# Chunk inputs by way of DRAM, and a new order of the mixer, in a hybrid decoder step

## The chip, the core and the metric

The kernel runs on one core of a Trainium2 chip. The metric is device microseconds of one execution, the median of several. PE is TensorE, DVE VectorE, ACT ScalarE, POOL GpSimd and SP SyncE, whose queue carries nearly all loads.

## The reference

One inference step of two trunk layers over 320 tokens (a prompt of 256 and eight samples of eight), each layer a half feed-forward, a mixer, a second half feed-forward and a gated input embedding:

```python
# Each layer (pre-RMSNorm everywhere, plain residual adds):
#   x += 0.5 * SwiGLU_1(rms(x))
#   z  = rms(x) @ w_in  -> [u (SSM_W) | q (ATTN_W) | k (KV_W) | v (KV_W)]
#   y_ssm  = GLU(Re(C h_t) + D u_t), h_t = Abar h_{t-1} + Bbar u_t   (32 groups x 16 ch, 64 complex states each)
#   y_attn = sliding-window (128) GQA with per-head sinks
#   x += concat(rms(y_ssm), rms(y_attn)) @ w_out
#   x += 0.5 * SwiGLU_2(rms(x))
#   x += (p[i] @ w_ple_proj) * sigmoid(rms(x) @ w_ple_gate)
def ssm_scan(u, h0, lam_re, lam_im, log_dt, b_re, b_im, c_re, c_im, d, w_glu):
    ...
    bu = jnp.einsum('gnp,blgp->lbgn', b_bar, ug)
    if h0 is not None:
        bu = bu.at[0].add(a_bar * h0)
    a = jnp.broadcast_to(a_bar, (l, SSM_G, SSM_N))
    _, h = lax.associative_scan(_ssm_combine, (a, bu), axis=0)
    y = jnp.einsum('gpn,lbgn->blgp', c, h).real.reshape(bt, l, SSM_W)
```

The scan is done in 40 chunks of eight tokens: what a chunk adds to the state (a product of its inputs with a table `wb` of powers), a scan over the chunks, and the output of a chunk from its own inputs (table `tt`) and from the state ahead of it (table `wc`).

## The kernel before

Features lie on the 128 partitions and the 320 tokens along the free axis. Every weight tile of 128x1024 is loaded by SP, and cut into a high half by ACT (L171, `wh`) and a low half by DVE (L172, `wl`); a product is three matmuls of 128x320 for each block of 128 rows (L206 to L208), 24 for one block of outputs. These long matmuls are nearly all that PE does.

`mix` does the mixer of one layer. A string of operations, `MIXSEQ`, is the order in which its code is written, and so the order of each engine's instructions; a scheduler then moves single instructions within what their tiles allow. A letter is an operation, its number the block: `p` and `q` the projections (`p0` to `p3` are u, 4 to 7 the queries, 8 and 9 key and value), `i` the chunk inputs, `r` the rotation, `v` the transposes of the value, `s` the scores and softmax of one pair of heads, `f` the transposes of the probabilities, `m` their product with the values, `y` the chunk output in its parts, `z` a product of the layer embedding, `t` and `w` loads of tables, `x` the load of the embedding, `g` the GLU, `A` and `S` the output projection.

- A projection ends in an evacuation by DVE that multiplies by the norm: u to `u2` (L682), queries (L686), key and value (L689, and an output `o_kvT` on POOL's queue, L690). PSUM has four kinds of buffers: `pc` (2), `pt` (3), `pa` (2), `po` (1). `p0` to `p7` but 2 and 3, and `z`, use `pc`; `p2`, `p3`, `p8`, `p9`, scores and transposes use `pt`.
- `chunk_in` (`i`) brings u of eight groups to chunk-major form: eight transposes of 128x40 (L699) in two halves, each copied to `X` by ACT (L82, tile `sx`), eight transposes of 40x128 (L704) of X, copied to `U` by ACT, and then 16 products with `wb` (L710), which ACT copies to `Vt`.
- `rotate` (`r`) is ten DVE instructions on eight groups: turn, scan over the chunks (L738), turn back, to `H` (L742) and `fin` (L743).
- `scores` (`s`) is for each of two heads two matmuls (L802, L804) and a masking on DVE (L805), then for the pair two reductions (L810), four exps on ACT (L812), a reciprocal (L814) and two products (L816). POOL writes the sinks ahead of it (L797). `flip` is six transposes (L827) and `mix` six products (L836). The tiles of `s` and of `rotate` take turns in two buffers.
- `y` is 16 products for eight groups (L923), two ACT copies to `sx`, eight transposes (L934) and a GELU on DVE and ACT (L936 to L946).

The tables are made by `prep`, whose steps lie beside the feed-forward ahead of the layer: powers of the state matrix in `pr`, `pi` (tiles `pwr`, `pwi`; POOL clears the first of each, L406, L407, behind a power function of its own, L427), `wc`, a table `tt` written to DRAM by eight copies on POOL's queue (L596, tile `ttd`), and `wb` (L605 to L627) from `q`.

```python
MIXSEQ = 'w0 q0 p3 i0 p2 i2 r0 w1 i3 r2 i1 p8 r3 r1 t1 p9 v t2 p5 t0 e x p4 y0 s0 s1 w2 f0 p6 m0 p7 s2 f1 t3 m1 s3 f2 m2 y0 w3 y0 y1 s4 f3 y1 m3 s5 z0 f4 z1 y1 z2 z3 y2 f5 y2 y3 m4 y3 y2 z4 y3 z5 z6 m5 a g0 g1 A0 n z7 A1 A2 S0 S1 S2 A3 S3'
ABUFS = {"s": 2, "p": 2, "qs": 1, "kc": 1, "vc": 1, "sx": 2, "pj": 1}
PBUFS = {"pa": 2, "pt": 3, "pc": 2, "po": 1}
```

## Time and profile before

| what | before |
|---|---|
| median of 3 runs | 1277.06 us (1277.05 to 1277.24) |
| the profiled execution's own time | 1276.93 us |
| its span | 1275.2 us |
| PE busy | 1257.2 us (99%) |
| DVE busy | 901.4 us (71%) |
| ACT busy | 602.0 us (47%) |
| POOL busy | 69.0 us (5%) |
| chain that ended last | PE 93%, DVE 3%, issue 2%, ACT 1% |
| POOL's queue | 2144 packets, 7.11 MB |
| SP's queue | 72992 packets, 198.50 MB |

The own time of the profiled execution is the span and what lies around it. A matmul's duration is longer than its distance to the next, since matmuls overlap: a long one is listed with 0.31 us, and starts 0.147 after the one ahead. What something costs on PE is read from starts, not from durations. A product of less than 128 rows or columns leaves two records for an instruction in some lines, so 16 products of L710 are 32 records. The mixer of layer 0 runs from 256.2 to 334.2, that of layer 1 from about 883.

### The profile page before, as it was taken

To read this page: it belongs to the slowest core of one execution; us is meant where nothing else is said; L and a number is where in the kernel's file an instruction comes from. 1 tells how busy PE (TensorE), PEld (TensorE's weight loads), DVE (VectorE), ACT (ScalarE), POOL (GpSimd) and SP (SyncE) were. 2 spreads that over 40 slices of the span, in tenths; PEclk is the share of its full clock that TensorE was granted. 3 is DMA by queue.
4 is the path that set the end of the run, shared out by engine and by line. 5 is a ranking of instruction groups with operands and counts; after the bars stand their busy time and mean duration, and the time that the engine had idled before them with its cause. 6 is when DMAs were issued, how large, how long until landed. Compare 5 with 4: busy or idle time off the path is not lost.

```text
span 1275.2 us, 23019 instructions
## 1 busy us (share of the span) xinstructions
PE 1257.2 (99%) x9167; PEld 1230.7 (97%) x9167; DVE 901.4 (71%) x1611; ACT 602.0 (47%) x995; POOL 69.0 (5%) x85
## 2 busy tenths in 40 slices
PE   9999999999999999999999999999999999999996
PEld 8999999988899999999999999999889999999996
DVE  7799677778779987766875555566977755555576
ACT  6443344556764433444654334445485543334454
POOL 2200200010104002000000000000000000000000
PEclk9999999999999999999999999999999999999998
DMA  7646855643254468655444354345422443444351
GB/s 242 216 123 193 298 205 180 229 165 122 77 179 162 128 188 298 222 196 156 167 158 151 117 165 166 131 124 190 177 105 98 151 149 125 147 175 143 114 174 42
DMA packets 75964, 208.72 MB, mean 164 GB/s; under 512 B 9664, under 2 KB 20544, under 8 KB 75856
## 3 DMA queue, kind: packets, MB, share of 16 engines
q1 hardware_dynamic: 72992, 198.50, 46.9%
q0 software_dynamic: 2144, 7.11, 1.5%
q8 instruction: 72, 1.18, 0.4%
q10 hardware_dynamic: 720, 1.64, 0.4%
q14 instruction: 36, 0.29, 0.1%
HBM read 193.62 MB, written 17.79 MB: 166 GB/s over the span
## 4 chain that ended last, share of the span: by engine, by line
PE 93%; DVE 3%; issue 2%; ACT 1%; DMA 0%; POOL 0%; POOLq 0%; SPq 0%; DVEq 0%; ACTq 0%
PE pt L206 18%; PE pt L207 18%; PE pt L208 17%; PE pc L206 11%; PE pc L207 11%; PE pc L208 11%; PE pa L923 1%; PE pa L623 1%; PE po L836 0%; PE pa L273 0%; DVE wl L172 0%; PE pt L827 0%; DVE s L734 0%; DVE s L733 0%; PE pa L934 0%
## 5 line engine op out<-in xcount | busy, mean ns | idle before, releaser
L171 ACT ACTIVATE wh<-wr 128x1024 fp32r<-128x1024 f32 (+3 forms) x370 | 351.9, 953 | 574.7 <-issue 276.7
L206 PE MATMUL pt<-big,wh 128*128 128x320 f32 x1584 | 491.8, 311 | 0.1
L207 PE MATMUL pt<-big,wh 128*128 128x320 f32 x1584 | 490.8, 310 | 0.0
L208 PE MATMUL pt<-big,wl 128*128 128x320 f32 x1584 | 490.3, 310 | 0.0
L172 DVE TENSOR_TENSOR wl<-wr,wh 128x1024 fp32r<-128x1024 f32 (+3 forms) x370 | 402.8, 1091 | 118.0 <-ACT wh L171 116.0
L206 PE MATMUL pc<-big,wh 128*128 128x320 f32 x984 | 307.5, 313 | 0.1
L207 PE MATMUL pc<-big,wh 128*128 128x320 f32 x984 | 305.2, 310 | 0.0
L208 PE MATMUL pc<-big,wl 128*128 128x320 f32 x984 | 305.1, 310 | 0.0
L206 PEld LDWEIGHTS pt<-big,wh 128*128 128x128 f32 x1584 | 297.6, 188 | 2.6 <-issue 1.2
L207 PEld LDWEIGHTS pt<-big,wh 128*128 128x128 f32 x1584 | 297.8, 188 | 0.9 <-DVE big L259 0.6
L208 PEld LDWEIGHTS pt<-big,wl 128*128 128x128 f32 x1584 | 297.7, 188 | 0.1
L206 PEld LDWEIGHTS pc<-big,wh 128*128 128x128 f32 x984 | 185.3, 188 | 1.7 <-issue 0.8
L208 PEld LDWEIGHTS pc<-big,wl 128*128 128x128 f32 x984 | 185.2, 188 | 0.4 <-issue 0.3
L207 PEld LDWEIGHTS pc<-big,wh 128*128 128x128 f32 x984 | 185.3, 188 | 0.3 <-issue 0.3
L322 DVE TENSOR_TENSOR fa<-pt,ft 128x320 f32<-128x320 f32 x88 | 43.1, 490 | 82.4 <-PE pt L208 82.2
L319 DVE TENSOR_TENSOR ft<-pc,r 128x320 f32<-128x320 f32 x87 | 42.2, 489 | 52.5 <-PE pc L208 52.3
L370 DVE SCALAR_TENSOR_TENSOR fd<-pt,r 128x320 f32<-128x320 f32 x64 | 31.5, 491 | 37.0 <-PE pt L208 37.0
L278 POOL TENSOR_TENSOR r<-ms,mhalf 107x3 f32<-107x3 f32 x13 | 15.6, 1202 | 622.8 <-DVE ms L276 622.8
L320 ACT ACTIVATE ft<-ft 128x320 f32<-128x320 f32 x88 | 40.0, 457 | 7.9 <-DVE ft L319 7.7
L327 DVE TENSOR_TENSOR big<-fa,big 128x320 fp32r<-128x320 f32 x88 | 42.7, 486 | 1.1 <-ACT big L326 1.1
L326 ACT ACTIVATE big<-fa 128x320 fp32r<-128x320 f32 x88 | 40.3, 459 | 5.7 <-DVE fa L322 5.3
L254 ACT ACTIVATE big<-xa,prm 128x320 fp32r<-128x320 f32 x64 | 35.5, 559 | 15.8 <-DVE xa L371 9.1
(252 smaller groups left out, 898.6 us busy)
## 6 DMA issues: line engine op xcount, KB each, us to landing
wr<-f2g SPq DMA_DIRECT2D x44, 512.0 KB, 3.3
wr<-f2u SPq DMA_DIRECT2D x44, 512.0 KB, 3.2
wr<-f1g SPq DMA_DIRECT2D x43, 512.0 KB, 3.3
wr<-f1u SPq DMA_DIRECT2D x43, 512.0 KB, 3.3
wr<-f1d SPq DMA_DIRECT2D x32, 384.0 KB, 3.1
wr<-f2d SPq DMA_DIRECT2D x32, 384.0 KB, 3.1
wr<-f1d SPq DMA_DIRECT2D x32, 320.0 KB, 2.9
wr<-win SPq DMA_DIRECT2D x20, 512.0 KB, 4.3
```

Source lines behind the costliest of these rows:

```text
L171: S.activation(h[:, c], raw[:, c], AF.Copy)
L172: lastwl.append(V.tensor_tensor(lo[:, c], raw[:, c], h[:, c].bitcast(F32), op=OP.subtract).ins)
L206: PE.matmul(ps, h[:, c], xh, start=start and k == 0, stop=False)
L207: PE.matmul(ps, h[:, c], xl, start=False, stop=False)
L208: mm = PE.matmul(ps, lo[:, c], xh, start=False, stop=stop and k == n - 1)
L254: S.activation(h, src, AF.Copy, scale=g)
L319: V.tensor_tensor(t, pg, r, op=OP.mult)
L320: S.activation(t, t, AF.Silu)
L322: V.tensor_tensor(a, pu, t, op=OP.mult)
L326: S.activation(h, a, AF.Copy)
L327: V.tensor_tensor(lo, a, h.bitcast(F32), op=OP.subtract)
L370: V.scalar_tensor_tensor(t, pd, 0.5, r, op0=OP.mult, op1=OP.mult)
```

## The change

1. `chunk_in` keeps only the 16 products with `wb` and the copy to `Vt`. The transposes L699 and L704 and the copies to X and U are gone. In their place a new operation `u`, `shuffle`, writes the four blocks of `u2` to a scratch tensor `ud` in DRAM, four copies of 160 KB, and reads it back into `U` in chunk-major form with eight copies, each to 16 partitions in 512 runs of 160 B. All twelve are on POOL's queue.
2. In U the order of the eight tokens of a chunk is turned, and so the rows of `tt` and the powers of `wb` are too. For that `prep` has 16 ACT copies that mirror `pr` and `pi` into `prr` and `pir`.
3. `MIXSEQ` is another. `u` follows p2 and p3; the projections p8, p9, p4 and p5, s0, f0, s1 and m0 stand ahead of the chunk products, which come in pairs around p6; the rotations follow, among the softmaxes.
4. `behind`: once a chunk product is written, the PE instructions of later `p`, `z` and `g` are held behind it in PE's order.

```diff
@@ -32,7 +32,7 @@
 STAT = (0, 107, 213)
 PF = 2
 WB = 4
-MIXSEQ = 'w0 q0 p3 i0 p2 i2 r0 w1 i3 r2 i1 p8 r3 r1 t1 p9 v t2 p5 t0 e x p4 y0 s0 s1 w2 f0 p6 m0 p7 s2 f1 t3 m1 s3 f2 m2 y0 w3 y0 y1 s4 f3 y1 m3 s5 z0 f4 z1 y1 z2 z3 y2 f5 y2 y3 m4 y3 y2 z4 y3 z5 z6 m5 a g0 g1 A0 n z7 A1 A2 S0 S1 S2 A3 S3'
+MIXSEQ = 'w0 q0 p2 p3 u p8 e p9 v p4 s0 p5 f0 i0 t0 r0 i1 w1 r1 p6 i2 t1 r2 s1 i3 w2 r3 x p7 m0 f1 y0 s2 y0 m1 y0 s3 t2 f2 y1 w3 m2 f3 y1 s4 m3 y1 z0 y2 t3 z1 f4 y2 z2 s5 z3 y2 f5 y3 m4 z4 y3 y3 z5 z6 m5 a g0 g1 A0 n z7 A1 A2 S0 S1 S2 A3 S3'
 ABUFS = {"s": 2, "p": 2, "qs": 1, "kc": 1, "vc": 1, "sx": 2, "pj": 1}
 PBUFS = {"pa": 2, "pt": 3, "pc": 2, "po": 1}
 KCUT = 7
@@ -592,14 +592,18 @@
             yield
         src = kt_d[l].rearrange("(p g) c -> p g c", g=G)
         for i in range(8):
-            dst = tt_d[l][(7 - i) * 16 : (8 - i) * 16, :].rearrange("p (g c) -> p g c", c=P)
+            dst = tt_d[l][i * 16 : i * 16 + 16, :].rearrange("p (g c) -> p g c", c=P)
             PO.dma_start(dst, src[:, :, (7 - i) * 16 : (7 - i) * 16 + P])
             if i % 4 == 3:
                 yield
-        V.tensor_copy(q[0:64, 0], pr[0:64])
-        V.tensor_copy(q[64:128, 0], pi[64:128])
-        V.tensor_scalar(q[0:64, 1], pi[0:64], -1.0, None, op0=OP.mult)
-        V.tensor_copy(q[64:128, 1], pr[64:128])
+        prr, pir = st("prr", (P, 8, G)), st("pir", (P, 8, G))
+        for k in range(8):
+            cp(prr[:, 7 - k], pr[:, k])
+            cp(pir[:, 7 - k], pi[:, k])
+        V.tensor_copy(q[0:64, 0, 0:8], prr[0:64])
+        V.tensor_copy(q[64:128, 0, 0:8], pir[64:128])
+        V.tensor_scalar(q[0:64, 1, 0:8], pir[0:64], -1.0, None, op0=OP.mult)
+        V.tensor_copy(q[64:128, 1, 0:8], prr[64:128])
         yield
         for gb in range(4):
             es = []
@@ -635,6 +639,8 @@
         groups = [0]
         tabs = {}
 
+        ud = dram.tile([4 * P, 8, NC], F32, name=f"ud{l}")
+
         def load(kind, gb):
             t = tabs[kind, gb] = tab.tile([P, 8, P], F32, name=nm(kind), tag="tab")
             src = {"wb": wb_d[l][gb], "wc": wc_d[l][gb], "tt": tt_d[l][:, gb * 1024 : (gb + 1) * 1024]}
@@ -690,26 +696,25 @@
                 PO.dma_start(O["kvT"][l, m - 8], t)
                 kv.append(t)
 
+        behind = []
+
+        def shuffle(k):
+
+            for gb in range(4):
+                drain(gb)
+                PO.dma_start(ud[gb * P : gb * P + P], u2[:, gb])
+            src = ud.rearrange("(g p) j c -> j p g c", p=16)
+            for j in range(8):
+                PO.dma_start(U[j * 16 : j * 16 + 16], src[j])
+
         def chunk_in(gb):
-            drain(gb)
-            X = auxt("sx", [NC, 8, 8, 16])
-            for hf in range(2):
-                px = pst("pa")
-                for s in range(4):
-                    PE.transpose(px[:NC, s * P : (s + 1) * P], u2[:, gb, 7 - (hf * 4 + s), :], ident)
-                cp(X[:, :, hf * 4 : hf * 4 + 4, :].rearrange("c g i p -> c i g p"),
-                   px[:NC].rearrange("c (i g p) -> c i g p", i=4, g=8))
-            pu = pst("pa")
-            for g in range(8):
-                PE.transpose(pu[:, g * NC : (g + 1) * NC],
-                             X[:, g].rearrange("c i p -> c (i p)"), ident[:NC, :NC])
-            cp(U[:, gb * 8 : gb * 8 + 8, :], pu[:, : 8 * NC].rearrange("p (g c) -> p g c", g=8))
             pv = pst("pa")
             for g in range(8):
                 for e in range(0, P, 64):
-                    PE.matmul(pv[e : e + 64, g * NC : (g + 1) * NC],
-                              tabs["wb", gb][:, g, e : e + 64], U[:, gb * 8 + g, :],
-                              start=True, stop=True)
+                    mm = PE.matmul(pv[e : e + 64, g * NC : (g + 1) * NC],
+                                   tabs["wb", gb][:, g, e : e + 64], U[:, gb * 8 + g, :],
+                                   start=True, stop=True)
+            behind[:] = [mm.ins]
             cp(Vt[:, gb * 8 : gb * 8 + 8, :], pv[:, : 8 * NC].rearrange("p (g c) -> p g c", g=8))
 
         gr, gi, ect, est, dec = gtab[l]
@@ -985,7 +990,7 @@
         un = [Prompt(m) for m in range(4)] + [Sample(0), Sample(1)]
         co = [chunk_out(gb) for gb in range(4)]
         ops = {
-            "p": proj, "q": proj2, "i": chunk_in, "r": rotate,
+            "p": proj, "q": proj2, "i": chunk_in, "u": shuffle, "r": rotate,
             "v": lambda k: attn_setup(), "s": lambda k: un[k].scores(),
             "f": lambda k: un[k].flip(), "m": lambda k: un[k].mix(),
             "y": lambda k: next(co[k], None), "g": glu,
@@ -996,7 +1001,8 @@
             "A": lambda k: wout("woa", k), "S": lambda k: wout("wos", k),
         }
         for o in seq:
-            ops[o[0]](int(o[1:] or 0))
+            with tc.issue_after(behind[0]) if behind and o[0] in "pzg" else nullcontext():
+                ops[o[0]](int(o[1:] or 0))
         shp = [P, G, 8]
         ft = auxt("s", [P, 2, G, 8])
         V.tensor_tensor(ft[:, 0], h0, gr.unsqueeze(2).to_broadcast(shp), op=OP.mult)
```

Lines from `load` on stand up to six further down in the new file (L710 is L714, L682 L688, L686 L692, L732 to L743 L737 to L748, L802 L807, L805 L810, L816 L821, L827 L832, L923 L928, L934 L939; L797 is L802).

On PE, ahead of a chunk product of layer 0 before (`pa_3258`, `pa_3264` the halves of X, `pa_3270` U of one block, `pt_3356` the key's projection):

```order
L699 MATMUL pa_3258<-ident,big_2998 40x128 [waits PE_49]
L699 MATMUL pa_3258<-ident,big_2998 40x128 x3
L207 MATMUL pt_3356<-big_2831,wh_3092 128x320
L699 MATMUL pa_3264<-ident,big_2998 40x128 [waits Activation_49]
L699 MATMUL pa_3264<-ident,big_2998 40x128 x3
L208 MATMUL pt_3356<-big_2830,wl_3093 128x320
L206 MATMUL pt_3356<-big_2830,wh_3092 128x320
L207 MATMUL pt_3356<-big_2831,wh_3092 128x320
L208 MATMUL pt_3356<-big_2830,wl_3093 128x320
L206 MATMUL pt_3356<-big_2830,wh_3092 128x320
L704 MATMUL pa_3270<-ident,sx_3257 128x40 [waits Activation_49]
L704 MATMUL pa_3270<-ident,sx_3257 128x40 x7
```

and at the first two chunk products now (`big_3018` is U, `big_3019` Vt, `pc_3432` the projection p6):

```order
L841 MATMUL po_3580<-p_3353,vtok_3032 64x128 x4
L841 MATMUL po_3580<-p_3353,vtok_3032 64x128 [waits Activation_49]
L841 MATMUL po_3580<-p_3353,vtok_3032 64x128
L714 MATMUL pa_3364<-big_3018,wb_3009 64x40 [waits DMASW5_49,DMASW4_49,DMASW6_49,DMASW3_49,DMASW7_49,DMASW2_49,DMAHW2_49,DMASW1_49,DMASW0_49]
L714 MATMUL pa_3364<-big_3018,wb_3009 64x40 x15
L714 MATMUL pa_3395<-big_3018,wb_3011 64x40 [waits DMAHW1_49]
L714 MATMUL pa_3395<-big_3018,wb_3011 64x40 x15
L206 MATMUL pc_3432<-big_2627,wh_3270 128x320
L207 MATMUL pc_3432<-big_2628,wh_3270 128x320
L208 MATMUL pc_3432<-big_2627,wl_3271 128x320
```

The products of i0 and i1 stand behind m0 (L841) and directly behind one another; the first waits for the reads from DRAM, the next long matmuls are p6's.

On DVE, the first rotation before (`s_3244`) stands among the evacuation of u (L682) and the cuts of weights:

```order
L172 TENSOR_TENSOR wl_3353<-wr_3350,wh_3352 128x1024 [waits DMAHW6_49,Activation_49]
L732 TENSOR_TENSOR s_3244<-big_3000,ect_877 128x256 [waits Activation_49]
L733 TENSOR_TENSOR s_3244<-big_3000,est_878 64x256
L734 TENSOR_TENSOR s_3244<-big_3000,est_878 64x256
L682 TENSOR_TENSOR big_2998<-pt_3177,r_3119 128x40x8 [waits PE_49]
L737 TENSOR_TENSOR s_3244<-s_3244 128x256 [waits DVE_49]
L172 TENSOR_TENSOR wl_3411<-wr_3408,wh_3410 128x1024 [waits DMAHW7_49,Activation_49]
L738 SCALAR_TENSOR_TENSOR s_3244<-dec_874,s_3244 128x256 [waits DVE_49,Pool_49]
L732 TENSOR_TENSOR s_3244<-s_3244,ect_877 128x256 [waits DVE_49]
L733 TENSOR_TENSOR s_3244<-s_3244,est_878 64x256
L734 TENSOR_TENSOR s_3244<-s_3244,est_878 64x256
L742 TENSOR_TENSOR big_3002<-s_3244 128x8x31 [waits DVE_49]
```

and the end of the third rotation now (`s_3478`), with the softmax of s1 (`s_3489`) and the evacuation of p7 (`pc_3554`):

```order
L810 SCALAR_TENSOR_TENSOR s_3489<-pt_3495,maskp 128x384
L743 SCALAR_TENSOR_TENSOR s_3478<-dec_874,s_3478 128x256 [waits DVE_49]
L815 TENSOR_REDUCE mneg_3499<-s_3489 128x2 [waits DVE_49]
L737 TENSOR_TENSOR s_3478<-s_3478,ect_877 128x256 [waits DVE_49]
L738 TENSOR_TENSOR s_3478<-s_3478,est_878 64x256
L739 TENSOR_TENSOR s_3478<-s_3478,est_878 64x256
L815 TENSOR_REDUCE mneg_3499<-s_3489 128x2
L747 TENSOR_TENSOR big_3021<-s_3478 128x8x31 [waits DVE_49]
L748 TENSOR_TENSOR fin_3022<-s_3478 128x8
L692 TENSOR_TENSOR big_3020<-pc_3554,r_3138 128x320 [waits PE_49]
L737 TENSOR_TENSOR s_3530<-big_3019,ect_877 128x256 [waits DVE_49,Activation_49]
L738 TENSOR_TENSOR s_3530<-big_3019,est_878 64x256
```

Rotations r0 to r2 and the maskings of s1 stand ahead of the evacuation of p7, and r3 (`s_3530`) behind it. On PE the second product of the embedding (`pc_3822`) takes the buffer of p7, and y0's transposes (L939) come behind it:

```order
L207 MATMUL pc_3802<-big_3543,wh_3428 128x320 [waits DVE_49]
L208 MATMUL pc_3802<-big_3543,wl_3429 128x320
L206 MATMUL pc_3822<-big_3543,wh_3428 128x320 [waits DVE_49]
L207 MATMUL pc_3822<-big_3543,wh_3428 128x320
L208 MATMUL pc_3822<-big_3543,wl_3429 128x320
L206 MATMUL pc_3822<-big_3543,wh_3428 128x320
L207 MATMUL pc_3822<-big_3543,wh_3428 128x320
L939 MATMUL pa_3653<-ident,sx_3601 128x40 [waits PE_49,Activation_49]
L939 MATMUL pa_3653<-ident,sx_3601 128x40 x7
```

On ACT, at the first SiLU (L320) of the first feed-forward before:

```order
L239 ACTIVATE sq_264<-xa 128x320 [waits DVE_49]
L171 ACTIVATE wh_391<-wr_389 128x1024 [waits DMAHW2_49,PE_49]
L320 ACT_TABLE_LOAD
L320 ACTIVATE ft_343<-ft_343 128x320 [waits DVE_49]
L171 ACTIVATE wh_446<-wr_444 128x1024 [waits DMAHW6_49,PE_49]
```

and now:

```order
L239 ACTIVATE sq_264<-xa 128x320 [waits DVE_49]
L171 ACTIVATE wh_391<-wr_389 128x1024 [waits DMAHW2_49,PE_49]
L82 ACTIVATE prr_1985<-pwr_434 128x32 [waits Pool_49]
L82 ACTIVATE pir_1986<-pwi_435 128x32 [waits Pool_49]
L320 ACT_TABLE_LOAD
L320 ACTIVATE ft_343<-ft_343 128x320 [waits DVE_49]
L171 ACTIVATE wh_446<-wr_444 128x1024 [waits DMAHW6_49,PE_49]
```

The first pair of mirroring copies stands ahead of the table load and waits for POOL.

## Rows read from the trace of the kernel before

**Rows 1.** Busy us by stretch (x records), granted clock, DMA share, GB/s: projections; the mixer's sum.

```profile
264.50:291.80 27.30, 26.53 (x287) 23.75 (x286) 24.10 (x51) 11.78 (x21) 2.60 (x4) 1.00 0.47 167
...
sum 78.00, PE 76.15 PEld 66.72 DVE 62.74 ACT 50.40 POOL 8.09; mean PE 15.23 PEld 13.34 DVE 12.55 ACT 10.08 POOL 1.62
```

**Rows 2.** Timeline of PE: start, duration, operation, records; p2 begins, then one chunk group.

```profile
256.69 0.39 PE L206 MATMUL pt<-big,wh 128*128 128x320 f32 x1
...
268.83 1.05 PE L699 MATMUL pa<-ident,big 128*40 128x128 f32 x8 [0.28 <-DVE big L682]
269.64 0.39 PE L207 MATMUL pt<-big,wh 128*128 128x320 f32 x1
269.87 0.31 PE L208 MATMUL pt<-big,wl 128*128 128x320 f32 x1
...
270.31 0.31 PE L208 MATMUL pt<-big,wl 128*128 128x320 f32 x1
270.67 0.69 PE L704 MATMUL pa<-ident,sx 40*128 40x40 f32 x8
271.29 0.41 PE L206 MATMUL pt<-big,wh 128*128 128x320 f32 x1
...
272.06 1.13 PE L710 MATMUL pa<-big,wb 128*64 128x40 f32 x32
```

**Rows 3.** Waits of PE from 256 to 334: total us, times, longest.

```profile
PE pt L827 <- DVE s L816: 0.6, 1, 0.6
PE pa L699 <- DVE big L682: 0.4, 2, 0.3
```

**Rows 4.** Timeline of DVE: a rotation's start, an evacuation within it, its last but one.

```profile
273.71 0.43 DVE L732 TENSOR_TENSOR s<-big,ect 128x256 f32<-128x256 f32 x1 [1.09 <-ACT big L82]
...
277.55 0.49 DVE L689 TENSOR_TENSOR kv<-pt,r 128x320 f32<-128x320 f32 x1
277.96 0.41 DVE L742 TENSOR_TENSOR big<-s 128x248 f32<-128x248 f32 x1
```

**Rows 5.** Timeline of DVE: masking, reductions and products of a softmax.

```profile
294.02 1.48 DVE L805 SCALAR_TENSOR_TENSOR s<-pt,maskp 128x384 f32<-128x384 f32 x3
295.42 1.01 DVE L810 TENSOR_REDUCE mneg<-s 128x2 f32<-128x514 f32 x2
...
298.31 1.03 DVE L816 TENSOR_TENSOR s<-s,dn 128x512 f32<-128x512 f32 x2
```

**Rows 6.** Timeline of ACT: first exps of two softmaxes, and a copy for `y`.

```profile
296.19 0.51 ACT L812 ACTIVATE s<-s,mneg 128x257 f32<-128x257 f32 x1 [3.35 <-DVE mneg L810]
...
297.97 0.50 ACT L812 ACTIVATE s<-s,mneg 128x257 f32<-128x257 f32 x1
...
310.21 0.58 ACT L82 ACTIVATE sx<-pa 40x512 f32<-40x512 f32 x1
```

**Rows 7.** Timeline of PE: eight products of `y` up to the first scores.

```profile
291.83 0.42 PE L923 MATMUL pa<-tt,big 128*40 128x128 f32 x4
...
292.83 0.71 PE L802 MATMUL pt<-kv,big 64*128 64x256 f32 x4
```

**Rows 8.** POOL's queue: landing of L690, issues (timeline) and landing of L596.

```profile
DMA to landing us min/median/max: 2.1/2.6/4.6
...
147.69 4.33 POOL L596 DMA_DIRECT2D ttd<-ktd  x7 [8.31 <-DMA ktd<-kc]
...
DMA to landing us min/median/max: 4.6/8.0/10.2
```

**Rows 9.** Timeline of ACT, POOL and PE near the first SiLU.

```profile
24.08 1.28 ACT L320 ACT_TABLE_LOAD   x1
28.05 0.47 ACT L320 ACTIVATE ft<-ft 128x320 f32<-128x320 f32 x1 [2.68 <-DVE ft L319]
...
32.65 0.13 POOL L407 MEMSET pwi<- 128x32 f32 x1
...
34.88 0.31 PE L206 MATMUL pt<-big,wh 128*128 128x320 f32 x1
```

## The prediction

> **What bounds the kernel now.** The change lies in the mixer of each layer, 78 us in layer 0 (256.2 to 334.2), so I read the busy time by stretch first [rows 1]: PE is busy for 76.15 of the 78, and time is won only where PE does less or stops waiting. DVE is busy for 24.10 of the 27.30 us in which the projections run and for 62.74 of the 78. It has the least to spare of the rest, and gets that far only because the four rotations lie under the projections. The timeline of PE around one chunk group [rows 2] gives the price of what goes; the waits of PE [rows 3] show that before hardly waits here. The runs' median is 1277.06; the profiled execution took 1276.93, with a span of 1275.2. I sum against 1276.93 and add the 0.13 at the end. A change under 0.2% (2.5 us) is more than a measurement of this kernel can tell from none: under 1274.5 is faster, over 1279.6 slower.
>
> **What goes from PE.** Of one chunk group the eight transposes of u take 268.83 to 269.64, 0.81 us, and the eight of X 270.67 to 271.29, 0.62 [rows 2]. The long matmuls are 0.147 apart (269.87 to 270.31 are three steps). PE leaves them at 270.31 and starts the second transposes 0.36 later, 0.21 more than a step, and from its first long matmul after the first transposes to the next it takes 0.23, 0.08 more. With a trip at 0.2 a group costs 0.81 + 0.62 + 2 x 0.2 = 1.8, four groups 7.3. As i0 and i1, and i2 and i3, now stand behind one another, two trips for the products go as well: 0.4. Two waits of before stand at places that the new order doesn't have, L699 for u2 and L827: 0.4 + 0.6 [rows 3]. Together 7.3 + 0.4 + 1.0 = **8.7 us per layer**. The ACT copies of X and U go too; ACT isn't what PE waits for there, and I count them at nothing.
>
> **What comes on PE.** The rotations can't begin before U is back and i0 has run. In the new order that is behind p8, p9, p4, p5, s0, f0, s1 and m0, some 20 us later than before, so that DVE idles under the projections and gets 17 us of rotations afterwards, among the softmaxes. Five places then hold PE up:
> - *z1*: its PSUM buffer is p7's, and p7's evacuation stands on DVE behind r0, r1 and r2. A rotation runs from 273.71 to 277.55 and, past an evacuation (0.41 to the next instruction), ends with the 0.41 at 277.96 [rows 4]: 4.25 with its last small write. From the end of i0's products: copy to Vt and handing over 0.6, three rotations 12.7, two evacuations and two 128x320 products of the layer embedding (0.41 each, as that evacuation) 1.6, s1's two maskings and two reductions (three maskings take from 294.02 to 295.42, two reductions 1.01) [rows 5] 1.9: together 16.8. PE meanwhile does i1 (1.1, as the 32 records at 272.06) [rows 2], p6 and p7 (48 x 0.147 = 7.1), i2 and i3 (2.2), y0 (16 instructions; eight take the 1.0 us from 291.83 to 292.83 [rows 7], so 2.0) and z0 (six matmuls, 0.9): 13.3. That is a wait of 3.5; with something for the hand-overs between two dozen dependent DVE instructions I take **3.8**.
> - *f0*: from s0's last score to its transposes lie masking 0.5, one reduction 0.6, four exps with their reads 1.8 (296.19 to 297.97) [rows 6], the reciprocal 0.2, the product 0.7 [rows 5] and hand-overs of about 0.5: 4.3, against 19 matmuls of p5 (2.8). **1.5**.
> - *s3*: its second score needs a PSUM buffer that s2's masking frees, on DVE behind r3, s1's products, y0's first GELU step and a cut of weights: 4.2 + 1.2 + 0.7 + 1.2, so 7.3, against 5.6 of PE's work (the rest of z, y1's transposes, f1, s2 and m1). **1.7**.
> - *y1's transposes*: the second copy of X' on ACT stands behind s2's four exps and a GELU step that waits for DVE: masking and reduction 1.5, exps 1.8, step 0.5, copy 0.6 [rows 6], 4.4 against some 2.1 of PE's. **2.3**.
> - *s1 and s2*: their second scores wait for ACT's copy of the turned probabilities, 0.3 each: **0.6**.
>
> Sum 9.9, against the 8.7 that go: **+1.2 per layer, +2.4 in all**. The bounds are wide, since no row shows the new order. If DVE and ACT hid all of it, the sum is -8.7 per layer; if DVE ran 6% behind my reckoning (3 us in the some 50 us that it has behind i0), it is about +4.
>
> **The trip through DRAM.** PE begins p2 at 256.69 [rows 2]; 48 long matmuls with one short trip end p3 near 264.5, the last of u2 is on DVE by 265.6, and its write is issued then. The nearest row is the key output of the same 160 KB on the same queue: 2.1 to 4.6 us to landing, median 2.6 [rows 8], which I take. All eight reads wait for that. They come with 512 runs each, as the ttd copies do, seven of which were issued in 4.33 us and which landed 4.6 to 10.2 after their issue [rows 8]; those runs are of 512 B, these of 160 B. Issues from 268.4 to 273 and a last landing 4.6 to 10.2 later give 277 to 283. PE reaches i0 at 264.5 + 96 x 0.147 and then v 0.5, s0 1.0, f0 0.8 with its wait 1.5, s1 1.3, m0 0.8 and five trips: some 285. So I count the trip at nothing, hidden under four projections with 2 to 8 us to spare; beyond a last landing of 12 us it costs one for one in both layers. The Trainium skill, "DMA: Bandwidth & Descriptors", Specifications, says that below 512 B a transfer falls short of line rate because the DMA engine reads, modifies and writes; if that doubled what lies between the first and the last landing of ttd, my estimate by that page is a last landing 15.8 us after issue and 1280 + 2 x 3.8 = 1288. No row here shows a stream of short runs: it stays a rival. On the same queue the key and value outputs and the sink copies of s1 to s3 stand behind the reads; s1's masking, the first to need one, comes over 10 us after the last read is issued.
>
> **The mirrored powers.** Sixteen ACT copies of 128x32 come with each layer's preparation, a few tenths each, and ACT has room for them. The first pair, though, stands on ACT ahead of the table load and the first SiLU of the first feed-forward, and waits for POOL's clearing of the power tables, over at 32.78 [rows 9]. Before, the load started at 24.08 and the SiLU at 28.05; now the SiLU comes at 32.8 + 0.4 + 1.28 = 34.5 at the earliest, and with its 0.47 and DVE's product behind it (some 0.5) the PSUM buffer that PE took at 34.88 comes free at 35.5: **0.6**, in layer 0. In layer 1 the pair stands in the second feed-forward of layer 0, whose buffers I take to cover it: nothing. The bounds are 0, if PE has another buffer, and the full shift of 6.4. `behind` only fixes where PE takes up the next projection and costs nothing but what stands above.
>
> Sum: 1276.93 + 2.4 + 0.6 + 0.13 = **1280**.
>
> **The rivals.**
> 1. *The waits don't add up.* DVE catches up, so that z1 and y1 wait half as long and f0 is covered. With 4.5 of the 9.9 left, each layer wins 4.2: 1277.06 - 8.4 + 0.6 = 1269.3; with none left 1277.06 - 17.4 + 0.6 = 1260.3. For it: every wait that I price is a difference of two long sums. Against: DVE's 62.74 of 78 [rows 1], with 20 us of it emptied.
> 2. *U lands late* (slower by a mechanism of its own). Four writes and eight reads of 160-B runs, one behind the other, land over 12 us after the last issue; at 16 us PE waits 4 us more in each layer, 1288; at 20, 1296. It decides from 12 on. For it: 4096 runs per layer beside the weights; against: ttd moved three times the bytes in its 10.2.
> 3. *ACT behind POOL*: the whole shift of 6.4 reaches PE, 1286. Against: that SiLU ended at 28.5, and what it freed was not used until 34.88.
> 4. *It doesn't do what it says*: PE's order is held by `behind`, the saved transposes turn into waits of the same length, and nothing is seen: 1277.
>
> **How the numbers follow.** My forecast (1276.5 to 1285) gets 0.47, rival 1 0.25, rival 2 0.13, rival 3 0.05, rival 4 0.10. Rival 1 is faster but for 0.01. Within 0.2% are rival 4 and 0.17 of the forecast, which lies only 0.4 above that line; the rest is slower. That is 0.24, 0.28 and 0.48. The range leaves out a tenth on either side: below 1267 the better part of rival 1, above 1289 the longer landings of rival 2.
>
> **What would show it.** Right: PE's waits name DVE's evacuation ahead of the embedding product (z1) with 3 to 5 us, L939 behind ACT with about 2, L832 behind L821; DVE nearly idle between the evacuation of p9 and U; i0's products not waiting for a DMA; the first SiLU near 34.5. Wrong: a wait of L714 for the reads (rival 2), a mixer that ends under 330 (rival 1), a gap of several us on PE near 35 (rival 3).

## The result, and the profile after

The changed kernel takes 1285.15 us, the median of five runs (1283.63 to 1290.4), beside 1277.06 for the kernel before: a ratio of 1.0071, with a 95% interval of 1.0060 to 1.0082. It is slower by some 8 us. The forecast was 1280, with a range of 1267 to 1289. The profiled execution took 1284.86, 7.93 more than that of before.

The page of the changed kernel: span, busy time of the engines, and the granted clock of TensorE in 40 slices.

```profile
span 1283.1 us, 22817 instructions
PE 1250.6 (97%) x9039; PEld 1228.0 (96%) x9039; DVE 896.6 (70%) x1611; ACT 592.0 (46%) x1003; POOL 78.5 (6%) x109
...
PEclk9999999998999999999999999999899999999998
```

PE is busy for 7 us less and the span is 8 us longer, so PE stands idle where it did not before. Of the 8s in the clock's row the first two lie in the two mixers; the third is the end of the span. The stretches of [rows 1], here of the changed kernel (length; busy time of PE, PEld, DVE, ACT, POOL; granted clock; DMA share; GB/s):

```profile
264.50:291.80 27.30, 24.97 (x235) 23.63 (x234) 16.16 (x27) 10.15 (x21) 6.70 (x11) 1.00 0.78 218
291.80:334.20 42.40, 37.54 (x405) 32.07 (x402) 36.52 (x87) 26.90 (x73) 1.98 (x6) 0.92 0.30 105
```

DVE does 16.16 under the projections, where it did 24.10, and behind them PE's clock averages 0.92. To split the 7.93 by place I use a step that POOL does once for each norm (L278). The second and the fifth of its thirteen enclose the mixer of layer 0, the eighth and the eleventh that of layer 1. Timeline of POOL, start and duration, the kernel before:

```profile
257.11 1.81 POOL L278 TENSOR_TENSOR r<-ms,mhalf 107x3 f32<-107x3 f32 x1 [43.59 <-DVE ms L276]
...
381.77 1.80 POOL L278 TENSOR_TENSOR r<-ms,mhalf 107x3 f32<-107x3 f32 x1 [30.03 <-DVE ms L276]
...
883.77 1.80 POOL L278 TENSOR_TENSOR r<-ms,mhalf 107x3 f32<-107x3 f32 x1 [42.77 <-DVE ms L276]
...
1008.30 1.80 POOL L278 TENSOR_TENSOR r<-ms,mhalf 107x3 f32<-107x3 f32 x1 [30.04 <-DVE ms L276]
```

And the changed kernel:

```profile
258.00 1.81 POOL L278 TENSOR_TENSOR r<-ms,mhalf 107x3 f32<-107x3 f32 x1 [38.68 <-DVE ms L276]
...
385.50 1.80 POOL L278 TENSOR_TENSOR r<-ms,mhalf 107x3 f32<-107x3 f32 x1 [31.01 <-DVE ms L276]
...
888.25 1.80 POOL L278 TENSOR_TENSOR r<-ms,mhalf 107x3 f32<-107x3 f32 x1 [42.78 <-DVE ms L276]
...
1016.21 1.80 POOL L278 TENSOR_TENSOR r<-ms,mhalf 107x3 f32<-107x3 f32 x1 [31.00 <-DVE ms L276]
```

The mixers went from 124.66 and 124.53 to 127.50 and 127.96: +2.84 and +3.43, where I forecast +1.2 each. From the first norm (25.55 before, 25.75 after) to the second it is 231.56 and 232.25, between the mixers 502.00 and 502.75: 0.69 and 0.75 more, where I forecast 0.6 and 0.

The waits of PE in the first of these spans of the changed kernel (total us, times, longest):

```profile
PE pc L206 <- DVE big L692: 2.7, 1, 2.7
PE pt L832 <- ACT wh L171: 2.3, 1, 2.3
PE pa L939 <- ACT sx L82: 2.2, 1, 2.2
PE pa L298 <- POOL r L278: 1.4, 2, 0.7
PE pt L206 <- ACT big L258: 0.5, 1, 0.5
PE po L904 <- ACT p L82: 0.4, 1, 0.4
PE pc L206 <- ACT gs L965: 0.2, 1, 0.2
```

They sum to 9.7; in layer 1 the first is 0.9 and L298 0.7, and the sum 7.2. The first three are z1, f0 and y1's transposes. Before, the same span had the two of [rows 3] and these, 2.5 in each layer:

```profile
PE pa L298 <- POOL r L278: 0.9, 1, 0.9
...
PE pt L760 <- DVE kv L689: 0.4, 1, 0.4
PE pt L802 <- DVE s L805: 0.2, 1, 0.2
```

The last piece is the clock. Three stretches of the changed kernel, with the granted clock as the number ahead of the DMA share:

```profile
300.00:312.00 12.00, 9.33 (x61) 7.42 (x62) 10.71 (x26) 6.35 (x18) 0.38 (x2) 0.72 0.37 130
...
914.00:924.00 10.00, 10.00 (x96) 9.45 (x96) 4.59 (x11) 2.33 (x6) 0.00 (x0) 0.50 0.48 145
...
948.00:951.00 3.00, 3.00 (x24) 2.44 (x23) 2.65 (x6) 0.81 (x3) 0.00 (x0) 0.50 0.46 175
```

In the kernel before it is 1.00 throughout both mixers, as in this stretch:

```profile
910.00:926.00 16.00, 15.34 (x114) 14.24 (x113) 15.07 (x32) 7.66 (x21) 2.10 (x3) 1.00 0.41 144
```

At 0.50 (1.2 GHz of 2.4) two long matmuls are 0.27 apart instead of 0.147. The three falls stand behind PE's waits at z1 (2.67, over at 302.95), at f0 of layer 1 (2.33, over at 913.20) and at y1's transposes of layer 1 (2.19, over at 947.72). The last two, on PE:

```profile
913.20 0.98 PE L832 MATMUL pt<-ident,s 128*128 128x128 f32 x6 [2.33 <-ACT wh L171]
...
947.72 0.95 PE L939 MATMUL pa<-ident,sx 40*128 40x40 f32 x8 [2.19 <-ACT sx L82]
```

By the three stretches PE lost 12 x 0.28 = 3.4 us in layer 0 and 10 x 0.50 + 3 x 0.50 = 6.5 in layer 1. The two of layer 1 lie within their falls: from 913 to 925 the mean clock is 0.57 and from 947 to 952 it is 0.66, which makes 6.9.

### The profile page after: what moved, and what is told of

Its sections match the earlier page's. It is cut to its first block, busy times and chain, and to the rows that moved or that the text cites. A ratio compares the mean times of both kernels' runs of the same rounds, so it can differ in the third digit from the quotient of the medians.

```text
span 1283.1 us, 22817 instructions
## 1 busy us (share of the span) xinstructions
PE 1250.6 (97%) x9039; PEld 1228.0 (96%) x9039; DVE 896.6 (70%) x1611; ACT 592.0 (46%) x1003; POOL 78.5 (6%) x109
## 4 chain that ended last, share of the span: by engine, by line
PE 86%; DVE 6%; issue 3%; ACT 2%; POOL 2%; DMA 1%; POOLq 0%; DVEq 0%; SPq 0%; ACTq 0%
PE pt L206 17%; PE pt L208 17%; PE pt L207 17%; PE pc L206 10%; PE pc L207 9%; PE pc L208 9%; DVE wl L172 2%; PE pa L928 1%; POOL dt L427 1%; ACT wh L171 1%; ACT s L817 1%; POOL r L278 1%; PE pt L832 1%; PE pt L807 1%; PE po L841 1%
## 5 line engine op out<-in xcount | busy, mean ns | idle before, releaser
L171 ACT ACTIVATE wh<-wr 128x1024 fp32r<-128x1024 f32 (+3 forms) x370 | 351.5, 952 | 523.5 <-issue 268.0
L320 ACT ACTIVATE ft<-ft 128x320 f32<-128x320 f32 x88 | 40.0, 458 | 25.1 <-DVE ft L319 24.9
L278 POOL TENSOR_TENSOR r<-ms,mhalf 107x3 f32<-107x3 f32 x13 | 16.3, 1250 | 549.1 <-DVE ms L276 549.1
```

The lines of the kernel that those rows point to most:

```text
L171: S.activation(h[:, c], raw[:, c], AF.Copy)
L320: S.activation(t, t, AF.Silu)
```

## The experiments

What each gave, with mixer 0 and 1 measured between the same steps of POOL. Kernels that stand beside the same time of the kernel before shared a chip with it. The ratio goes by the means of the runs, so it can differ a little from the quotient of the medians. The mixers, and all waits and clocks below, are those of the one profiled execution, which isn't always a typical one: in e4 and e6 it was the slowest (1301.03 and 1273.81), in e5 the fastest (1280.29).

| kernel | median us | before | ratio (95%) | mixers |
|---|---|---|---|---|
| the changed kernel | 1285.15 | 1277.06 | 1.0071 (1.0060 to 1.0082) | 127.50, 127.96 |
| e1_pair_const | 1285.10 | 1276.81 | 1.0059 (1.0047 to 1.0072) | 128.48, 128.09 |
| e2_mirror_alone | 1279.52 | 1276.81 | 1.0016 (1.0007 to 1.0025) | 124.89, 124.55 |
| e3_scores_behind | 1270.81 | 1276.81 | 0.9958 (0.9945 to 0.9970) | 122.00, 121.50 |
| e4_transposes_back | 1295.42 | 1276.81 | 1.0145 (1.0121 to 1.0170) | 135.78, 135.98 |
| e5_fill | 1281.84 | 1277.26 | 1.0032 (1.0021 to 1.0043) | 126.12, 125.10 |
| e6_short_turn | 1267.97 | 1277.26 | 0.9931 (0.9912 to 0.9950) | 122.42, 122.07 |
| e7_second_hop | 1289.53 | 1277.26 | 1.0090 (1.0075 to 1.0105) | 129.54, 131.98 |
| e8_six_tables | 1272.70 | 1277.26 | 0.9960 (0.9947 to 0.9974) | 123.06, 123.09 |
| e9_s1_fill | 1276.22 | 1277.07 | 0.9995 (0.9987 to 1.0004) | 125.44, 123.30 |
| e10_p7_early | 1279.34 | 1277.07 | 1.0015 (1.0006 to 1.0023) | 125.07, 124.98 |
| e11_p7_f0fill | 1276.06 | 1277.51 | 0.9990 (0.9981 to 0.9999) | 122.21, 122.53 |
| e12_p7_f0fill_pair | 1275.18 | 1277.51 | 0.9980 (0.9970 to 0.9990) | 123.85, 122.66 |

**The mirrored powers.** Once without the first pair's copies, and once alone, on the kernel before:

```diff
-        for k in range(8):
+        PO.memset(prr[:, 7], 1.0)
+        PO.memset(pir[:, 7], 0.0)
+        for k in range(1, 8):
             cp(prr[:, 7 - k], pr[:, k])
```

> The changed kernel with one thing taken away: the first of the eight mirrored power pairs (a one and a zero) is written by two GpSimd memsets instead of two ScalarE copies, so no copy stands ahead of the first SiLU's table load. My theory: PE starts the first mixer 0.9 us late and loses 0.75 us more between the layers because ScalarE waits there for GpSimd; both go, so the mixer of layer 0 starts where it did before (its norm's power function at 257.1 instead of 258.0) and the time falls by some 1.5 us, to about 1283.6. Rival (the delay ahead of the mixer comes from the other fourteen copies or from elsewhere): the mixer still starts at 258.0 and the time stays at 1285.

```diff
+        for k in range(8):
+            cp(prr[:, 7 - k], pr[:, k])
+            cp(pir[:, 7 - k], pi[:, k])
...
-                    PE.transpose(px[:NC, s * P : (s + 1) * P], u2[:, gb, 7 - (hf * 4 + s), :], ident)
+                    PE.transpose(px[:NC, s * P : (s + 1) * P], u2[:, gb, hf * 4 + s, :], ident)
```

> The kernel before with only the mirrored tables of the change (order of the tokens in U, tt and wb turned, sixteen ScalarE copies in each preparation); transposes and order of the mixer as before. My theory: 0.9 us ahead of the first mixer and 0.75 between the layers, so 1278.5 to 1278.8, and the mixers as long as before (124.7 us from the norm's power function at the mixer's start to the next-but-two, in both layers). Rival (the mirroring costs nothing by itself): 1277.1.

Both say the same of the pair. Alone it lengthens the two feed-forward stretches to 232.24 and 502.80, by 0.7 and 0.8. Without its first copies they are 231.55 and 502.06, as before. The median of e1 did not follow, though: in its profiled execution the mixers are longer by 1.0 and 0.1, and the granted clock fell at another place as well, to a mean of 0.76 from 280 to 287, behind the f0 wait of layer 0. By the ratios e1 is 0.12% faster, which would be the pair, but the intervals overlap, and the totals settle nothing. So the pair's 1.4 us are shown by the stretches, and the clock's falls are worth as much.

**What the order costs.** The trip kept, and the order of before around it: chunk products and rotations ahead of the softmaxes (pair as in e1).

```diff
-MIXSEQ = 'w0 q0 p2 p3 u p8 e p9 v p4 s0 p5 f0 i0 t0 r0 i1 w1 r1 p6 i2 t1 r2 s1 i3 w2 r3 x p7 m0 ...
+MIXSEQ = 'w0 q0 p2 p3 u w1 p8 p9 v e x p4 p5 i0 t0 r0 i1 r1 p6 p7 i2 t1 r2 i3 r3 t2 y0 s0 s1 w2 f0 m0 ...
```

> The changed kernel with the trip through DRAM kept and the mixer's order turned back: chunk products directly behind p8, p9, p4 and p5, rotations beside p6 and p7, all scores behind them as in the kernel before; the first mirrored pair constant as in e1_pair_const. My theory (late rotations make DVE the bound, the trip itself is hidden or nearly): no wait for p7's evacuation or for f0, PE waits up to 1 us for the reads of U and some 3 us at a score, the clock stays up; the removed transposes show as a gain, 1266 to 1270. Rival 1 (the trip or GpSimd's queue costs the time): PE waits for the reads for several us in each layer, 1280 or more. Rival 2 (the transposes were worth nothing): about 1277.

1270.81, just above the range given, and the fastest here of the kernels that compute everything: 0.42% under the kernel before. Its mixers are 2.7 and 3.0 under those of the kernel before and 5.5 and 6.5 under those of the changed kernel. So bringing the inputs by way of DRAM is worth having in this order, and the new order is what spoils it (`behind` is the same in both kernels, and so isn't to blame; what it costs by itself was not tried). That it is the rotations in the new order, this run can't tell from the place of the softmaxes; e6_short_turn does below. The longest wait left is one for a table, and the clock still falls once in each mixer:

```profile
PE pa L930 <- DMA tt<-ttd: 2.2, 1, 2.2
```

A sixth buffer for the tables was to take it away:

```diff
-    tab = ctx.enter_context(tc.tile_pool(name="tab", bufs=5))
+    tab = ctx.enter_context(tc.tile_pool(name="tab", bufs=6))
```

> The kernel of e3_scores_behind (DRAM trip kept, chunk products and rotations ahead of the softmaxes) with a sixth buffer for the chunk tables; prr and pir move into another scratch buffer to make room. What was left there of waits was the table tt (3.6 us of PE's waits, longest 2.2, whose load was issued late for want of a buffer), with a fall of the granted clock behind it. Theory (a late table is a wait that a buffer takes away): the load is issued earlier, PE doesn't wait for tt, the clock stays up, and the mixers lose 1 to 2 us each: 1266 to 1269.5. Rival (the load is late because SP's queue is full of weights, whatever the buffer): 1270 to 1272.

The wait for the table went, and one of 2.3 for DVE's masking of s0, ahead of s1's second score, came in both layers. The time (1272.70) is above both ranges and not under e3_scores_behind's. In DVE's order that masking stands behind most of the last two rotations, so the wait for the table had hidden that DVE was late. Filling that new wait:

```diff
+                    if m == 1 and k == 0:
+                        xh = pj_now["pairs"][0][0]
+                        for _ in range(13):
+                            PE.matmul(ps[:, :T], xh[:, :P], xh, start=True, stop=True)
```

> The kernel of e8_six_tables with 13 extra 128x320 matmuls (1.9 us) ahead of the first score of s1, into the PSUM tile that the score overwrites; they take the place of PE's wait of 2.30 us for DVE's masking ahead of s1's second score, and everything else stands as it did. [...]

A miss of the experiment: the fill was to take the place of the wait, but the trace has the extra matmuls ahead of the last chunk products (which begin at 291.52 instead of 289.94), so that the rotations begin later and the wait stays at 2.3. Nor are its 3.5 us over e8_six_tables a clean price of the fill, since the clock fell at other places in the two profiled executions. The run is inconclusive.

**Whether the trip through DRAM costs.** The new order with the transposes back on PE and no trip, and then the trip made longer by a second hop:

```diff
-MIXSEQ = 'w0 q0 p2 p3 u p8 ...
+MIXSEQ = 'w0 q0 p2 p3 p8 ...
...
+            for hf in range(2):
+                px = pst("pa")
+                for s in range(4):
+                    PE.transpose(px[:NC, s * P : (s + 1) * P], u2[:, gb, hf * 4 + s, :], ident)
...
```

> The changed kernel with its order and mirrored tables, but with the chunk inputs transposed on PE as before and no trip through DRAM. My theory (the order costs, not the trip): the rotations are as late as in the changed kernel or later, PE does 7 to 9 us more work per layer, of which only what falls into its waits is hidden: 1285 to 1300, no faster than the changed kernel. Rival (the trip through DRAM or its queue is what costs): the time falls back to 1277 to 1280.

1295.42, 10 us slower than the changed kernel, with runs from 1289.8 to 1301.03: what the trip takes off PE is a gain, in this order too. How much of the 10 is work and how much the clock, the total doesn't tell: in the profiled execution the clock is lower for longer as well (0.51 from 286 to 299).

```diff
-                PO.dma_start(ud[gb * P : gb * P + P], u2[:, gb])
+                PO.dma_start(ue[gb * P : gb * P + P], u2[:, gb])
+            for gb in range(4):
+                PO.dma_start(ud[gb * P : gb * P + P], ue[gb * P : gb * P + P])
```

> The changed kernel with a second hop of the chunk inputs through DRAM: four more copies of 160 KB, DRAM to DRAM, between the writes and the eight reads. That makes U late on purpose, by the landing of one more copy (2.6 to 3.4 us, by the four writes) and four issues. In the changed kernel the last read landed at 278.5 and i0 begins at 285.88, so 7.4 us are to spare. Theory (the trip is hidden, with those 7.4): U lands at 282 to 284, no wait at the chunk products, time as the changed kernel's, 1283 to 1287. Rival (the trip already costs, by traffic beside the weights or by U just in time): 3 to 10 us more, 1288 to 1296, and a wait of L715 for a DMA.

1289.53, 4.4 above the changed kernel and in the rival's range. My expectation was wrong by its own arithmetic. In the changed kernel the eight reads are issued from 270.47 on, one every 0.63 us; I had added the longest landing to the first issue. The last two of them landed after 7.6 and 8.0. Issue of the reads on POOL, the landing of the last two, and i0 on PE, in the changed kernel:

```profile
270.47 5.04 POOL L708 DMA_DIRECT2D big<-ud  x8 [3.63 <-ACT wh L171]
...
DMA to landing us min/median/max: 7.6/7.8/8.0
...
285.88 0.84 PE L714 MATMUL pa<-big,wb 128*64 128x40 f32 x23
```

So U was there at some 282.5 and PE came at 285.88: 3.4 us to spare, not 7.4. With the second hop the last read is issued at 283.24 and lands at 288.1, and PE waits for it. Last issue, its landing, and i0:

```profile
283.24 0.63 POOL L711 DMA_DIRECT2D big<-ud  x1 [0.59 <-DMA big<-ud]
...
DMA to landing us min/median/max: 4.9/4.9/4.9
...
288.32 0.98 PE L717 MATMUL pa<-big,wb 128*64 128x40 f32 x14 [1.00 <-DMA big<-ud]
```

U is 5.6 later, 3.4 of that was to spare and PE itself was 1.4 late: 0.8, against a wait of 1.0. So in layer 0 the trip of the changed kernel is hidden, with a margin of 3.4 us, and beyond that the wait grows about one for one. In layer 1 the wait at i0 is 1.5. The mixers grew by more than these waits, 2.0 and 4.0: the clock loses 5.1 us in mixer 0 instead of 3.4, and z1's wait in layer 1 is 2.7 instead of 0.9.

**What the late rotations cost.** The turns left out of the rotations:

```diff
-            turn(v)
-            V.tensor_tensor(t, t, w, op=OP.subtract)
...
-            turn(g)
```

> The changed kernel with the rotations cut short: of the ten DVE instructions the two turns are left out, so that the scan and the small writes remain; the state is thereby not turned and this part of the computation is missing. A rotation takes then about 1 us of DVE, not 4.25. Theory (what holds PE up in the new order are DVE's late rotations): the waits at z1 and s3 go, those of y1 and f0, which stand behind a softmax, mostly stay; 3.3 x 4 = 13 us of DVE per mixer fall away, the mixers come from 127.5 and 128.0 to 120 to 123.5 and the total to 1270 to 1276. Rival (PE waits for the softmax chain and ACT, not for the rotations): within 2 us of the changed kernel, 1283 to 1286.

The mixers came down by 5.1 and 5.9, in the slowest of the four runs, whose clock still falls behind f0 in both layers (a mean of 0.57 from 283 to 295). Of the waits, z1's is gone, that of y1's transposes is 0.9 instead of 2.2, and f0's is the same:

```profile
PE pt L830 <- ACT wh L171: 2.3, 1, 2.3
PE pa L937 <- ACT sx L82: 0.9, 1, 0.9
```

The median, 1267.97, is below the 1270 expected, and 17 under the changed kernel. So the rotations on DVE are what holds PE up at z1 and in part at y1's transposes, but not at f0. Then one operation moved, so that p7's evacuation stands on DVE ahead of the last two rotations:

```diff
-... w1 r1 p6 i2 t1 r2 s1 i3 w2 r3 x p7 m0 ...
+... w1 r1 p6 p7 i2 t1 r2 s1 i3 w2 r3 x m0 ...
```

> The changed kernel with one operation of the order moved: p7 directly behind p6, ahead of the last two rotations and of i2 and i3, so that its evacuation no longer stands on DVE behind r2 and r3. Theory (z1 waits for a PSUM buffer that this evacuation frees): the wait of 2.67 us at the embedding product is gone, and in layer 0 the fall of the clock behind it; the f0 wait of 2.33 stays, as does that of y1's transposes in part, since both hang on softmaxes. Mixer 0 goes from 127.5 to 121.5 to 125, mixer 1 from 128.0 to 123 to 127, total 1275 to 1281. Rival (DVE sets the pace, whatever stands first on it): the wait turns up elsewhere, s3 or y1, with 2 to 3 us, total 1283 to 1287.

As the theory has it: z1's wait is gone, f0's is 2.33, y1's is split in two of at most 0.9, the mixers lose 2.4 and 3.0, and 1279.34 lies in the range given. The rival, that the wait only moves, falls. But the clock falls behind the f0 wait in both layers now, as in this stretch:

```profile
280.00:300.00 20.00, 17.67 (x158) 16.52 (x158) 12.66 (x29) 7.54 (x19) 0.00 (x0) 0.74 0.38 126
```

**What the clock costs.** Idle places of PE filled with matmuls of no use, first in the changed kernel ahead of f0's and y1's transposes:

```diff
+                    if self.m == 0 and n == 1:
+                        for _ in range(13):
+                            PE.matmul(pp[:, :T], xs[0][0][:, :P], xs[0][0], start=True, stop=True)
...
+            if gb == 1:
+                xh = pj_now["pairs"][0][0]
+                for _ in range(12):
+                    PE.matmul(po[:, :T], xh[:, :P], xh, start=True, stop=True)
```

> The changed kernel with idle places of PE filled: 13 extra 128x320 matmuls ahead of f0's transposes and 12 ahead of y1's, into PSUM tiles that the transposes overwrite, so nothing of the result hangs on them; at 0.147 us each (1.9 and 1.8 us) they take the place of the waits of 2.33 and 2.19 us. z1's wait stays as it is. Theory (what makes the mixers 1.6 and 2.2 us longer than my sum is the granted clock, which falls to 0.5 after PE has waited over 2 us): the stretches at 0.5 behind f0 and behind L939 in layer 1 (about 914 to 924 and 948 to 951) are gone, mixer 1 goes from 127.96 to 126 to 127.5, and the total is 0 to 3 us under the changed kernel: 1282 to 1285. Rival (PE's slower stretch lies in time that DVE would take anyway): clock near 1.00 and mixer 1 within 0.3 of 127.96. Second rival (the fill costs its own length because the waits come in addition): mixers 3 to 4 us longer, 1292.

1281.84, just under what the clock theory gave, and 3.3 under the changed kernel. The f0 and y1 waits shrink to 0.4 each, z1's is 2.7 in both layers, and the only falls are behind z1. Two stretches of it:

```profile
300.00:312.00 12.00, 9.39 (x77) 7.68 (x78) 11.78 (x30) 6.34 (x18) 1.47 (x2) 0.86 0.32 124
910.00:926.00 16.00, 15.57 (x216) 14.45 (x215) 12.10 (x30) 6.76 (x16) 0.37 (x1) 1.00 0.57 193
```

With 25 matmuls more in each mixer, mixer 1 is 2.9 us shorter than without them. No wait got cheaper: the fill takes 3.7 and saves 3.7 of f0's and y1's, and z1's wait is 1.8 longer. Only the clock is left to have brought the gain. (In that mixer the rows gave a loss of 6.5 to 6.9; the one fall that is left, behind z1, costs 1.7.) The same fill ahead of f0 in e10_p7_early (13 matmuls of the first lines above):

> The kernel of e10_p7_early with the f0 wait filled as in e5_fill: 13 extra 128x320 matmuls (1.9 us) ahead of f0's transposes, into the tile that these overwrite. In e10_p7_early the granted clock falls to 0.5 for 10.24 us behind that wait in each layer, the only fall in its mixers. Clock theory (at 0.5 PE does half, and what it loses there the mixer loses): the clock stays at 1.00 in both mixers, the f0 wait shrinks from 2.33 to under 0.6, and the mixers come from 125.07 and 124.98 to 119.5 to 121.5, total 1268 to 1273. Rival (the slow stretch only hid that DVE is late with the rotations, so that PE, now on time, waits for DVE instead): a wait of 2 us or more for DVE at the embedding product, at s3 or at y1's transposes, mixers 123 to 125, total 1275 to 1280.

```profile
280.00:300.00 20.00, 19.46 (x258) 18.13 (x256) 15.46 (x34) 10.33 (x25) 0.18 (x1) 1.00 0.42 148
300.00:320.00 20.00, 16.53 (x193) 14.54 (x194) 19.63 (x47) 14.09 (x46) 0.67 (x2) 1.00 0.43 154
```

Mixer 0 keeps its clock from end to end, and is 2.9 shorter than without the fill. Mixer 1 doesn't: its clock falls once, behind a wait of 1.5 for the table `tt`. The 2.9 are short of the 3.6 to 5.6 expected: PE, on time again, comes sooner to the table `tt`, and waits for it. So the rival had a share, by a DMA and not by DVE:

```profile
PE pa L931 <- DMA tt<-ttd: 1.6, 1, 1.6
```

Over eleven runs the median is 1276.06, above the clock theory's range and in the rival's; the runs go from 1272.92 at a mean clock of 0.997 to 1279.67 at 0.992. With the first mirrored pair as constants on top:

```diff
-        for k in range(8):
+        PO.memset(prr[:, 7], 1.0)
+        PO.memset(pir[:, 7], 0.0)
+        for k in range(1, 8):
```

> The kernel of e11_p7_f0fill with the first mirrored pair written as constants by GpSimd, as in e1_pair_const, where 0.69 and 0.75 us of the two feed-forward stretches fell away. Expected: both stretches as in the kernel before (231.56 from the first to the second norm step, 502.0 between the mixers), and 1.4 us under e11_p7_f0fill; if the clock stays up in its mixers, 1266.5 to 1271.5, which is about the time of e3_scores_behind. Rival (the shift in time changes when the clock falls, as in e1_pair_const): the two stretches shorten and the mixers lengthen by as much or more, total at or above e11_p7_f0fill.

The two stretches are back at 231.57 and 501.99, but mixer 0 has a wait of 2.7 for the table and a fall behind it. 1275.18 is 0.9 under e11_p7_f0fill, not 1.4, so neither range was met, and some 3 to 4 above e3_scores_behind: the fill takes away the fall behind the wait that it fills, but doesn't do what the better order does.

## Why the prediction was right, and where it was not

The time lay in the range and the sign was the forecast one. The places of the main waits and the work that goes were right as well. But the sum is 5 us short, and that the sign came out right was luck: without a loss for which the sum has no term, the measured parts come to a little faster or no change, as shown below. e11_p7_f0fill has a mixer 0 with the clock at 1.00 throughout. Its 122.21, less its listed waits of 6.2 and its fill of 1.9, leaves 114.1 of PE's work; the kernel before has 124.66 - 2.5 = 122.2. So the changed kernel's mixer, which does the same work in nearly the same order as that of e11_p7_f0fill, is 8.1 us lighter. That gives this account of the two profiled executions:

| part | us | from |
|---|---|---|
| ahead of the first norm | +0.2 | 25.55, 25.75 |
| mirrored pair | +1.4 | 0.69 and 0.75 |
| PE's work in the mixers | -16.2 | twice 8.1 |
| listed waits | +11.9 | 9.7 + 7.2, against twice 2.5 |
| what is left of the mixers: the clock | +10.4 | 127.50 - 123.8 and 127.96 - 121.3 |
| sum | +7.7 | measured 7.93 |

The 10.4 is a remainder, but the granted clock's rows give nearly the same without it: 3.4 + 6.5 = 9.9, or 10.3 with the wider stretches. The Trainium skill, "TensorE: Matmul & The Clock Gate", Terms, puts such a penalty at the time spent at the lower level times the share of clock missing; the trace agrees, with 9.9 to 10.3 by that rule and 10.4 by the account.

- **What goes from PE.** Forecast 7.7 of work (7.3 and two trips of 0.2) and 1.0 of waits per layer; 8.1 of work went, and 1.6 of waits. The transposes were well priced from [rows 2].
- **z1.** Forecast 3.8, measured 2.67. From the end of i0's products (some 286.9) to p7's evacuation I gave DVE 16.8 and it took 16.0; PE took 13.4 for what I gave 13.3. The cause is the named one: e10_p7_early moves that evacuation, and the wait is gone. DVE's evacuation and PE's first product behind it, the first long ones at half clock:

```profile
302.41 0.48 DVE L692 TENSOR_TENSOR big<-pc,r 128x320 f32<-128x320 f32 x1
...
302.95 0.63 PE L206 MATMUL pc<-big,wh 128*128 128x320 f32 x1 [2.67 <-DVE big L692]
303.38 0.47 PE L207 MATMUL pc<-big,wh 128*128 128x320 f32 x1
303.64 0.47 PE L208 MATMUL pc<-big,wl 128*128 128x320 f32 x1
```

- **f0.** Forecast 1.5, measured 2.33. I had the softmax begin with the masking when the scores are there; on DVE a cut of weights of 1.23 stands ahead of it. That accounts for the 0.8 missing. The wait bears the name of L171 on ACT, but the transposes read the products of the softmax (L821); the chain is masking, exps, products. DVE, ACT and PE:

```profile
277.09 1.23 DVE L172 TENSOR_TENSOR wl<-wr,wh 128x1024 fp32r<-128x1024 f32 x1 [0.45 <-ACT wh L171]
278.23 1.02 DVE L810 SCALAR_TENSOR_TENSOR s<-pt,maskp 128x384 f32<-128x384 f32 x2
...
280.07 0.51 ACT L817 ACTIVATE s<-s,mneg 128x257 f32<-128x257 f32 x1 [3.01 <-DVE mneg L815]
...
282.18 1.03 DVE L821 TENSOR_TENSOR s<-s,dn 128x512 f32<-128x512 f32 x2
...
283.02 0.85 PE L832 MATMUL pt<-ident,s 128*128 128x128 f32 x6 [2.33 <-ACT wh L171]
```

- **y1's transposes.** Forecast 2.3, measured 2.19 in both layers, by the chain I named: s2's exps, a GELU step, then the second of the two copies to `sx` on ACT. ACT, then PE:

```profile
314.70 0.50 ACT L817 ACTIVATE s<-s,mneg 128x257 f32<-128x257 f32 x1
...
316.94 0.59 ACT L82 ACTIVATE sx<-pa 40x512 f32<-40x512 f32 x1
...
317.59 0.69 PE L939 MATMUL pa<-ident,sx 40*128 40x40 f32 x8 [2.19 <-ACT sx L82]
```

- **s3, s1 and s2.** Forecast 1.7 and 0.6; no such wait is listed, in the changed kernel or in mixer 0 of e11_p7_f0fill, where PE isn't slowed. These terms, 2.3 together, were wrong.
- **The trip.** Forecast hidden with 2 to 8 us to spare, U at 277 to 283; measured 282.5 and 3.4. The longest landing was 8.0, under the 12 from which rival 2 decides. The doubling that made my estimate by the Trainium skill, "DMA: Bandwidth & Descriptors", Specifications, 15.8 was an assumption of mine, since that section gives no factor. This case's trace shows no doubling: in layer 0 the copies with 512 runs of 160 B landed in 3.5 to 8.0, those with as many runs of 512 B, and so over three times the bytes, in 4.6 to 10.2 [rows 8].
- **The pair.** Forecast 0.6 in layer 0, measured 0.69; in layer 1 I let the buffers cover it and it costs 0.75 (e2_mirror_alone: 0.8). ACT's load and SiLU of the changed kernel, beside [rows 9], and PE:

```profile
33.33 1.28 ACT L320 ACT_TABLE_LOAD   x1
34.63 0.47 ACT L320 ACTIVATE ft<-ft 128x320 f32<-128x320 f32 x1
...
35.68 0.41 PE L206 MATMUL pt<-big,wh 128*128 128x320 f32 x1 [0.43 <-DVE fa L322]
```

- **The step that failed** is the one behind "Sum 9.9, against the 8.7 that go": it takes a wait of PE to cost its own length and no more. The waits themselves came out smaller than forecast: listed waits rose by 7.2 in layer 0 and 4.7 in layer 1, against a net 8.9 forecast. By the account without the clock, the mixers would be 123.8 and 121.3, or 123.1 with z1's full wait in layer 1: with the pair that is 1274 to 1276, faster by a little or no change (an estimate). Rival 1, that the waits don't add up, was right only in that they are fewer: f0 is not covered, and z1 of layer 0 and y1 do not wait half as long as forecast (2.67 and 2.19, against 3.8 and 2.3). z1 of layer 1 does (0.9), but behind a PE that was slowed ahead of it; where e5_fill keeps the clock up there, it is 2.7. What made the kernel slower is what the waits do behind them: some 10 us lost at the lower level of the clock, for which the sum had no term.

Rival 2 falls: no wait of L714 for the reads is listed. Rival 3 falls too, though its premise came: the first SiLU starts 6.6 later (34.63, against 28.05 before), but PE waits 0.43 there and the stretch is 0.7 longer. Of rival 4 the outcome is near in layer 0, where 8.1 of work went and listed waits rose by 7.2; its mechanism falls, since e6_short_turn and e10_p7_early take such waits away with `behind` in place, and e4_transposes_back shows that the transposes were worth taking off PE. What stays open is when a wait is followed by a fall: the f0 wait of 2.33 was in layer 1 of the changed kernel and not in layer 0, and in both layers of e10_p7_early.

## What to carry to other kernels

When work is taken off the bounding engine, look where the work that was hidden under it goes: here the rotations lost the projections that covered them, and with the same trip through DRAM the kernel is 0.7% slower with them late and 0.4% faster with them early (there with the first mirrored pair as constants). In the changed kernel three waits of two to three microseconds had some 10 us of lost clock behind them, more than their own 7.2, so price such a wait with the slow stretch behind it, and look at the granted clock before explaining a difference by work. When the wait for one thing is removed, read the trace for what comes late next: the sixth table buffer brought nothing.
